# A hybrid encoder on one core: another PSUM bank for the pool sums, four mixer weights split early, GpSimd's work beside the recurrence moved to VectorE and ScalarE

## The chip, the core and the metric

The kernel runs on one core of a Trainium2 chip. Its engines are TensorE (PE, matmuls; PEld is its weight load), VectorE (DVE), ScalarE (ACT), GpSimd (POOL) and SyncE (SP, which here only issues DMAs). The metric is the device time of one execution in microseconds (us).

## The reference

A two-layer encoder for 256 tokens of width 1024, all in float32. Each layer is a mixer and a feed-forward part. The mixer makes one input projection and gives its columns to three head groups; their outputs are concatenated, projected back and added:

```python
h = rmsnorm(x, norm_mix[l])
proj = h @ w_in_first                      # layer 1: w_in_rest, with 32 more columns, v_down
u_rwkv, q, k, v, u_pool = split_cols(...)
y_a, v_first = rwkv7_mixer(u_rwkv, ...)    # bidirectional recurrence, 4 heads x 64
y_b = diff_attention(q, k, v, ...)         # partial rotary, 4 heads
y_c = pool_mixer(u_pool, ...)              # centred means over windows 2, 4, 8, 16
x = x + concatenate([y_a, y_b, y_c]) @ w_out[l]
x = x + (swiglu(h2, ffn...) if l == 0 else moe_swiglu(h2, router, exp...))   # h2 = rmsnorm(x)
```

In the recurrence `us = u + mu0 * (prev - u) + mu1 * (next - u)` is the shifted input. A decay `w` and a rate `a` come from two small low-rank projections (here "LoRA") of it, `kk` is the normalised key, and in layer 1 the value is mixed with that of layer 0: `v = v + (v_first - v) * sigmoid(vres_bias + v_down @ vres_up)` (the value residual). The feed-forward part of layer 0 is a dense SwiGLU (width 3584), that of layer 1 a mixture of 8 such experts.

## The kernel before, in words

**Stages.** Mixer 0 runs to 202 us of the span, the dense feed-forward part to 438, mixer 1 to 628, the experts to 1544.

**A weight's way.** A matmul in float32 precision is made of three passes on rounded operands (`mm3`): high by high, high by low, low by high. Each weight tile of 128x1024 (512 KB) therefore goes through `wload` (L184): SP loads `raw` (a ring of 4 slots), ACT rounds it to `whi` (L201, the "cast"), and DVE, or for the loads whose index is in `POOLW` GpSimd, computes `wlo = raw - whi` (L209, the "split"). `whi` and `wlo` have rings of 3 slots, so the split of a later weight waits until the matmuls of an earlier one are through. `self.spare` holds extra tiles that come ahead of the ring. They are parts of tiles which the mixer needs only later (`qk`, `qT`, `kT`), under the same tags. In layer 0 there are two, in layer 1 none. The index counts the mixer's loads after the first projection: in mixer 0, 0 and 1 are the two pool weights p0 and p1, 2 to 5 are q0 to q3, then k0 and so on; in mixer 1, 0 is `v_down`, 1 and 2 are p0 and p1, 3 to 6 are q0 to q3.

**A mixer up to the first Gram.** The first projection fills four PSUM banks (`pa`). DVE scales each into `u` (L552), and `us` is made of it with an ACT or GpSimd product and two DVE instructions for each of 8 columns (L546 to L550). PE then makes the LoRA products (`ps<-us,lora`), and between these and what follows the pool sums (p0, p1) and the projection q (q0 to q3). From the LoRA products DVE makes the scans of the decay (L631, L633). PE's sums of k squared (`ps<-consts,ksq`) go through DVE and GpSimd (`rn`, L621, L622) to `ksq` (L624), are transposed on PE and give `kk` (L642), `kd` (L659), `bb` (L657) and with the exponentials of the scans `Wd` and `IW` the operands `AR` (L655, and L656 on GpSimd) and `BK` (L665, L666). The Gram matmuls of direction 0 (`ps<-AR,BK`) need all of these for direction 0; the recurrence follows behind them.

**The order.** PE's order is written by hand: the parts of a mixer are generators which are woven, each `yield LAT[i]` being the modelled time after which the generator may go on. On the other engines a scheduler of the framework orders the instructions, so an edit can move instructions that it doesn't name.

**The value residual** (`vres`, mixer 1) and the pool sums both take a bank of tag `pq`. `vres` stands ahead of the pool sums in `proj`; behind its wait `LAT[15]` come the `vup` matmuls, a tanh on ACT, and four GpSimd instructions (L1038 to L1041).

## Time and profile before

| | |
|---|---|
| three runs, us | 1544.89, 1545.96, 1548.17; median 1545.96 |
| the profiled execution, us | 1545.79, of which the span of the profile is 1544.0 |
| PE busy | 1458.9 us, 94% of the span |
| DVE busy | 1002.7 us, 65% |
| ACT busy | 808.8 us, 52% |
| POOL busy | 176.5 us, 11% |
| DMA | 434.67 MB, 282 GB/s on average, about 410 GB/s in the experts |

The shares are averages over stages with different limits, so the stage must be looked at by itself.

### The profile page before, as it was taken

What the parts mean: (1) busy time and instruction counts of PE and PEld (TensorE: products, weight loads), DVE (VectorE), ACT (ScalarE), POOL (GpSimd) and SP (SyncE); (2) the same over time, 40 slices, a digit from 0 to 9 for tenths busy, and PEclk for the clock granted to TensorE, in tenths of its full rate; (3) what the DMA queues carried; (4) which work ended last, traced back from release to release, by engine and by line L of the source; (5) the groups of instructions that cost most, each with busy time, mean ns of one, the idle gap of its engine ahead of it and who ended that gap; (6) DMA issues with size and microseconds to landing.
All of it is one profiled execution on the core that took longest, in us unless ns stands there. A gap on an engine that the chain in (4) does not pass through costs nothing.

```text
span 1544.0 us, 27158 instructions
## 1 busy us (share of the span) xinstructions
PE 1458.9 (94%) x10215; PEld 1105.8 (72%) x10215; DVE 1002.7 (65%) x1314; ACT 808.8 (52%) x1142; POOL 176.5 (11%) x161
## 2 busy tenths in 40 slices
PE   6899989999998899899999999999999999998996
PEld 6777889999986768688743688888634787435885
DVE  4875665555659746799620898999512898206896
ACT  4545464444445354588510777777302776205785
POOL 2532100000026332400000000010000010000001
PEclk9899999999998899999999999999999999999998
DMA  7322255666543236779799999999999999999990
GB/s 228 108 71 98 98 176 178 190 190 187 170 121 96 61 135 247 259 275 363 283 413 414 411 411 411 411 388 339 368 419 411 410 411 417 409 416 411 410 411 36
DMA packets 172457, 434.67 MB, mean 282 GB/s; under 512 B 14834, under 2 KB 18013, under 8 KB 172317
## 3 DMA queue, kind: packets, MB, share of 16 engines
q1 hardware_dynamic: 170924, 430.74, 75.1%
q8 instruction: 82, 1.34, 0.3%
q0 software_dynamic: 544, 1.12, 0.3%
q10 hardware_dynamic: 848, 0.99, 0.3%
q14 instruction: 59, 0.48, 0.1%
HBM read 431.75 MB, written 1.05 MB: 280 GB/s over the span
## 4 chain that ended last, share of the span: by engine, by line
PE 73%; DMA 10%; DVE 10%; ACT 3%; issue 2%; POOL 1%; ACTq 0%; SPq 0%; DVEq 0%; POOLq 0%
PE ps L226 70%; DMA r<-in_exp_up 6%; PE ps L230 3%; DMA r<-in_exp_gate 2%; DVE wlo L209 1%; DVE wlox L209 1%; DMA lamk<-in_lambda_k 1%; ACT whi L201 1%; DMA r<-in_exp_down 1%; ACT whix L201 1%; DVE us L550 1%; DVE us L549 0%; DMA x<-in_x 0%; DVE BK L665 0%; ACT Sf L761 0%
## 5 line engine op out<-in xcount | busy, mean ns | idle before, releaser
L209 DVE TENSOR_TENSOR wlo<-r,whi 128x1024 fp32r<-128x1024 f32 x193 | 233.5, 1237 | 43.2 <-ACT whi L201 36.7
L201 ACT CAST whi<-r 128x1024 fp32r<-128x1024 f32 x196 | 202.6, 1054 | 37.3 <-DMA r<-in_exp_gate 18.5
L209 DVE TENSOR_TENSOR wlox<-r,whix 128x1024 fp32r<-128x1024 f32 x125 | 152.2, 1237 | 62.7 <-ACT whix L201 56.1
L201 ACT CAST whi<-raw 128x1024 fp32r<-128x1024 f32 x123 | 129.3, 1053 | 94.5 <-PE ps L226 82.8
L209 DVE TENSOR_TENSOR wlo<-raw,whi 128x1024 fp32r<-128x1024 f32 x108 | 137.2, 1273 | 56.5 <-ACT whi L201 56.0
L201 ACT CAST whix<-r 128x1024 fp32r<-128x1024 f32 x125 | 130.2, 1056 | 39.4 <-DMA r<-in_exp_gate 26.8
L226 PE MATMUL ps<-whi,gf 128*128 128x512 f32 x396 | 133.5, 395 | 0.0
L226 PE MATMUL ps<-r,gs 128*64 128x512 f32 (+1 forms) x636 | 131.1, 549 | 1.7 <-DMA r<-in_exp_up 1.7
L226 PE MATMUL ps<-fT,whi 128*128 128x256 f32 x544 | 98.5, 284 | 4.7 <-DVE gu L1306 3.8
L226 PE MATMUL ps<-whix,gf 128*128 128x512 f32 x276 | 95.3, 399 | 2.6 <-ACT whix L201 2.6
L226 PEld LDWEIGHTS ps<-r,gs 128*64 128x64 f32 x636 | 42.6, 136 | 72.4 <-issue 58.0
L1417 POOL TENSOR_TENSOR xp<-x,xp 128x512 fp32r<-128x512 f32 x12 | 22.3, 1858 | 626.9 <-ACT xp L1416 581.0
L226 PEld LDWEIGHTS ps<-fT,whi 128*128 128x128 f32 x544 | 84.4, 191 | 6.0 <-issue 4.3
L226 PEld LDWEIGHTS ps<-whi,gf 128*128 128x128 f32 x396 | 74.4, 188 | 18.2 <-issue 1.6
L1663 ACT COPY mah<-ps 128x512 f32<-128x512 f32 (+1 forms) x12 | 6.4, 532 | 139.5 <-PE ps L230 139.5
L226 PE MATMUL ps<-wlo,gf 128*128 128x512 f32 x198 | 78.1, 394 | 0.3 <-DVE wlo L209 0.2
L226 PE MATMUL ps<-fT,wlo 128*128 128x256 f32 x272 | 76.9, 283 | 0.0
L226 PE MATMUL ps<-whi,hT_h 128*128 128x512 f32 x160 | 70.4, 440 | 5.7 <-DVE up L1073 5.6
L209 DVE TENSOR_TENSOR wlox<-raw,whix 128x1024 fp32r<-128x1024 f32 x49 | 61.2, 1251 | 17.7 <-ACT whix L201 17.6
L226 PE MATMUL ps<-whi,mah 128*128 128x512 f32 x170 | 66.5, 391 | 0.0
L226 PE MATMUL ps<-wlo,hT_h 128*128 128x512 f32 x160 | 65.7, 410 | 0.8 <-DVE wlo L209 0.8
L226 PE MATMUL ps<-wlo,mah 128*128 128x512 f32 x170 | 66.4, 390 | 0.0
(460 smaller groups left out, 3376.7 us busy)
## 6 DMA issues: line engine op xcount, KB each, us to landing
r<-in_exp_gate SPq DMA_DIRECT2D x184, 512.0 KB, 10.0
r<-in_exp_up SPq DMA_DIRECT2D x173, 512.0 KB, 9.9
r<-in_exp_down SPq DMA_DIRECT2D x171, 512.0 KB, 10.1
raw<-in_exp_down SPq DMA_DIRECT2D x48, 512.0 KB, 10.0
raw<-in_exp_up SPq DMA_DIRECT2D x43, 512.0 KB, 10.0
raw<-in_exp_gate SPq DMA_DIRECT2D x34, 512.0 KB, 10.0
raw<-in_w_in_first SPq DMA_DIRECT2D x22, 512.0 KB, 4.4
raw<-in_w_in_rest SPq DMA_DIRECT2D x22, 512.0 KB, 3.7
```

What stands on the lines that cost most here:

```text
L201: w1 = nc.scalar.copy(hi[:, :a * b], raw[:, :a * b])
L209: w2 = (early or nc.vector).tensor_sub(lo[:, :a * b], raw[:, :a * b], hi[:, :a * b].bitcast(F32))
L226: self.nc.tensor.matmul(out, lhsT, rhs, start=start, stop=stop, skip_group_check=skip_group_check)
L230: self.nc.tensor.transpose(out, in_, ident)
L550: nc.vector.scalar_tensor_tensor(us[:, f, :T - 1], b[:, 1:], m1, us[:, f, :T - 1], op0=ALU.mult, op1=ALU.add)
L1417: nc.gpsimd.tensor_sub(xl, xs, xh.bitcast(F32))
L1663: nc.scalar.copy(at, b)
```

## The change

Four edits, all in the mixers:

- `POOLW` loses 5 and 6: the splits of q3 and k0 in mixer 0, of q2 and q3 in mixer 1, go from GpSimd to DVE.
- The spare tiles are now four for each of `whi` and `wlo`, in both layers: for `whi` the tile of tag `qk` and the first halves of `kT`, `AR` and `bkuv`, for `wlo` that of `qT` and the second halves. So the first four weights behind the first projection (p0, p1, q0, q1 in mixer 0; `v_down`, p0, p1, q0 in mixer 1) no longer wait for a slot of the ring, and `AR` and `BK` of the recurrence now wait for the matmuls of the weights that lie in their tiles.
- The pool sums take a bank of tag `at` instead of `pq`, and the `vup` matmuls of the value residual, with all that hangs on them, are written behind the pool sums instead of ahead of them.
- The zero halves of `kT` are written by ACT (a copy with scale 0) instead of by two GpSimd memsets.

```diff
-POOLW = (5, 6, 9, 12, 13, 14, 16, 22, 23)
+POOLW = (9, 12, 13, 14, 16, 22, 23)
...
-        if l == 0:
-
-            kT = P.tile([128, 2, 1024], F32R, name="kTs", tag="kT")
-            self.spare = {n: [P.tile([128, 1024], F32R, name=t_ + "s", tag=t_), kT[:, i_]]
-                          for i_, (n, t_) in enumerate((("whi", "qk"), ("wlo", "qT")))}
+
+        two = [P.tile([128, 2, 1024], F32R, name=t_ + "s", tag=t_) for t_ in ("kT", "AR", "bkuv")]
+        self.spare = {n: [P.tile([128, 1024], F32R, name=t_ + "s", tag=t_)] + [t2[:, i_] for t2 in two]
+                      for i_, (n, t_) in enumerate((("whi", "qk"), ("wlo", "qT")))}
...
-        yield LAT[15]
+        yield
         b = self.bank("pq")
...
-        if l > 0:
-            yield from self.vres(l, P, S["us"], hh, hl, wk)
-
-        pbk = self.bank("pq")
+        vres = self.vres(l, P, S["us"], hh, hl, wk) if l else iter(())
+        next(vres, 0)
+
+        pbk = self.bank("at")
...
+        next(vres, 0)
         self.S["up"] = up = P.tile([128, 3, 2, T + 2 * POOL_PAD], F32, name="up", tag="BKt")
...
-                nc.gpsimd.memset(tT[64:128, 0], 0.0)
-                nc.gpsimd.memset(tT[0:64, 1], 0.0)
+                for m in range(2):
+                    h = slice(64 - 64 * m, 128 - 64 * m)
+                    nc.scalar.activation(tT[h, m], self.rst[h, None, :].to_broadcast([64, 4, T]), AF.Copy, scale=0.0)
```

What the scheduler makes of it is seen in the order of the engines. DVE's queue in mixer 0, from the split of p1 (into `kTs`) on, before (`wlo_608` is of q0, `wlo_646` of q1; `ps_172` to `ps_175` are the four banks of the first projection):

```order
L209 TENSOR_TENSOR kTs<-raw_573,kTs 128x1024
L209 TENSOR_TENSOR wlo_608<-raw_606,whi_607 128x1024
L372 TENSOR_TENSOR ang<-ang 128x16
L373 TENSOR_SCALAR cos<-ang 128x16
L552 TENSOR_TENSOR u<-ps_172,R 128x512
L209 TENSOR_TENSOR wlo_646<-raw_644,whi_645 128x1024
L549 SCALAR_TENSOR_TENSOR us<-u,vecs,us 128x255
L552 TENSOR_TENSOR u<-ps_173,R 128x512
```

and with the change (`ARs` and `bkuvs` are the spare tiles, of q0 and q1; line numbers here are one lower):

```order
L209 TENSOR_TENSOR kTs<-raw_575,kTs 128x1024
L209 TENSOR_TENSOR ARs<-raw_608,ARs 128x1024
L372 TENSOR_TENSOR ang<-ang 128x16
L209 TENSOR_TENSOR bkuvs<-raw_644,bkuvs 128x1024
L373 TENSOR_SCALAR cos<-ang 128x16
L551 TENSOR_TENSOR u<-ps_172,R 128x512
L551 TENSOR_TENSOR u<-ps_173,R 128x512
L551 TENSOR_TENSOR u<-ps_174,R 128x512
L551 TENSOR_TENSOR u<-ps_175,R 128x512
L548 SCALAR_TENSOR_TENSOR us<-u,vecs,us 128x255 x2
```

The split of q1 moved ahead of the first scaling `u`, and the four scalings stand together.

DVE's queue in mixer 1, from the split of the first projection's weight number 6 on, before (`wlo_5132` is of its last weight, number 7, `wlo_5162` of `v_down`, `wlo_5169` of p0):

```order
L209 TENSOR_TENSOR wlo_5102<-raw_5100,whi_5101 128x1024
L209 TENSOR_TENSOR wlo_5132<-raw_5130,whi_5131 128x1024
L209 TENSOR_TENSOR wlo_5162<-raw_5160,whi_5161 128x1024
L552 TENSOR_TENSOR u<-ps_4909,R 128x512
L209 TENSOR_TENSOR wlo_5169<-raw_5167,whi_5168 128x1024
L549 SCALAR_TENSOR_TENSOR us<-u,vecs,us 128x255
L552 TENSOR_TENSOR u<-ps_4910,R 128x512
```

and with the change (`qTs` is of `v_down`, `kTs` of p0, `wlo_5130` of weight 7, `ARs` of p1, `bkuvs` of q0, `wlo_5400` of q1):

```order
L209 TENSOR_TENSOR wlo_5100<-raw_5098,whi_5099 128x1024
L209 TENSOR_TENSOR qTs<-raw_5163,qks 128x1024
L209 TENSOR_TENSOR kTs<-raw_5168,kTs 128x1024
L209 TENSOR_TENSOR wlo_5130<-raw_5128,whi_5129 128x1024
L209 TENSOR_TENSOR ARs<-raw_5299,ARs 128x1024
L209 TENSOR_TENSOR bkuvs<-raw_5363,bkuvs 128x1024
L209 TENSOR_TENSOR wlo_5400<-raw_5398,whi_5399 128x1024
L551 TENSOR_TENSOR u<-ps_4907,R 128x512
L551 TENSOR_TENSOR u<-ps_4908,R 128x512
```

Two splits now stand ahead of that of weight 7, and three more ahead of the first `u`.

GpSimd's queue in mixer 1, from its last product of `us` to the sum of `kd`, before:

```order
L1039 TENSOR_TENSOR vdf<-vfirst,us 128x512
L813 TENSOR_SCALAR sg<-us 128x2x2x64
L1038 TENSOR_SCALAR vsig<-vsig 128x512
L1040 TENSOR_TENSOR vdf<-vdf,vsig 128x512
L1041 TENSOR_TENSOR us<-us,vdf 128x512
L809 COPY vs<-us 128x4x2x64
L656 TENSOR_TENSOR AR<-us,Wd 128x8x64
L673 COPY wcx<-Wd 128x2 x3
L622 TENSOR_TENSOR rn<-rn,dvecs 128x8
L656 TENSOR_TENSOR AR<-us,Wd 128x8x64
L209 TENSOR_TENSOR wlo_5469<-raw_5467,whi_5468 128x1024
L209 TENSOR_TENSOR wlo_5487<-raw_5485,whi_5486 128x1024
```

and with the change:

```order
L1038 TENSOR_TENSOR vdf<-vfirst,us 128x512
L812 TENSOR_SCALAR sg<-us 128x2x2x64
L655 TENSOR_TENSOR AR<-us,Wd 128x8x64
L621 TENSOR_TENSOR rn<-rn,dvecs 128x8
L672 COPY wcx<-Wd 128x2 x3
L655 TENSOR_TENSOR AR<-us,Wd 128x8x64
L672 COPY wcx<-Wd 128x2 x3
L1037 TENSOR_SCALAR vsig<-vsig 128x512
L1039 TENSOR_TENSOR vdf<-vdf,vsig 128x512
L1040 TENSOR_TENSOR us<-us,vdf 128x512
L808 COPY vs<-us 128x4x2x64
L675 TENSOR_TENSOR kd<-kd 128x512
```

The two splits are gone from it, and the value residual's instructions went behind the `AR` products and `rn`. From the first Gram on, the orders of all engines agree but for a few places, and SP's agrees throughout.

## Rows read from the trace of the kernel before

**Rows 1.** The page: the span, and ACT's casts (count, busy, mean ns).

```profile
span 1544.0 us, 27158 instructions
...
L201 ACT CAST whi<-raw 128x1024 fp32r<-128x1024 f32 x123 | 129.3, 1053 | 94.5 <-PE ps L226 82.8
```

**Rows 2.** Windows: length; busy of PE, PEld, DVE, ACT, POOL; granted clock; DMA.

```profile
42.30:72.50 30.20, 22.69 (x115) 18.82 (x113) 28.23 (x40) 16.35 (x32) 20.70 (x19) 0.86 0.30 89
71.00:77.60 6.60, 5.12 (x33) 4.93 (x33) 5.74 (x10) 0.00 (x0) 1.88 (x2) 0.50 0.28 82
464.60:498.80 34.20, 26.84 (x146) 22.57 (x144) 32.37 (x42) 20.14 (x36) 23.20 (x20) 0.85 0.30 91
498.80:502.10 3.30, 3.27 (x33) 3.18 (x34) 3.30 (x6) 0.00 (x0) 1.27 (x1) 1.00 0.56 162
628.00:1544.00 916.00, 881.95 (x4081) 598.55 (x4079) 602.50 (x634) 509.29 (x617) 39.93 (x24) 0.99 0.95 371
```

**Rows 3.** Chain of waits, 40 to 80 us: start, length, what.

```profile
68.02 2.77 DVE AR L655
```

**Rows 4.** Timeline of DVE in mixer 0: start, length, what, idle before and its releaser.

```profile
41.30 0.68 DVE L552 TENSOR_TENSOR u<-ps,R 128x512 f32<-128x512 f32 x1
42.44 1.30 DVE L209 TENSOR_TENSOR wlo<-raw,whi 128x1024 fp32r<-128x1024 f32 x1 [0.45 <-ACT whi L201]
...
52.75 1.26 DVE L631 TENSOR_TENSOR_SCAN cs<-rst,cs 128x256 f32<-128x256 f32 x2
...
60.56 1.41 DVE L624 COPY ksq<-rn 128x512 f32<-128x512 f32 x1 [1.79 <-POOL rn L622]
61.89 0.68 DVE L659 TENSOR_TENSOR kd<-kd,us 128x512 f32<-128x512 f32 x1
...
63.21 2.88 DVE L659 TENSOR_TENSOR kd<-kd,us 128x512 f32<-128x512 f32 x1
...
67.94 2.85 DVE L655 TENSOR_TENSOR AR<-kk,Wd 128x512 f32<-128x512 f32 x1
```

**Rows 5.** Timeline of POOL in mixer 0.

```profile
62.70 2.84 POOL L209 TENSOR_TENSOR wlo<-raw,whi 128x1024 fp32r<-128x1024 f32 x1
```

**Rows 6.** Timeline of PE in mixer 0.

```profile
46.08 2.83 PE L226 MATMUL ps<-us,lora 128*128 128x256 f32 x12 [0.87 <-issue]
...
57.07 1.49 PE L226 MATMUL ps<-consts,ksq 128*128 128x2 f32 x8
...
72.47 5.10 PE L226 MATMUL ps<-AR,BK 64*128 64x128 f32 x32 [3.84 <-DVE BK L665]
```

**Rows 7.** Timeline of DVE in mixer 1.

```profile
458.75 1.23 DVE L209 TENSOR_TENSOR wlo<-raw,whi 128x1024 fp32r<-128x1024 f32 x1 [1.49 <-ACT whi L201]
...
464.60 0.69 DVE L552 TENSOR_TENSOR u<-ps,R 128x512 f32<-128x512 f32 x1 [1.30 <-PE ps L226]
...
478.40 3.38 DVE L631 TENSOR_TENSOR_SCAN cs<-rst,cs 128x256 f32<-128x256 f32 x2
...
489.89 2.74 DVE L666 TENSOR_TENSOR BK<-kd,IW 128x512 f32<-128x512 f32 x1
...
496.09 2.93 DVE L665 TENSOR_TENSOR BK<-bb,IW 128x256 f32<-128x256 f32 x2
```

**Rows 8.** Groups of DVE's instructions, 464.6 to 498.8 us: count, busy, mean ns, idle.

```profile
L209 DVE TENSOR_TENSOR wlo<-raw,whi 128x1024 fp32r<-128x1024 f32 x4 | 4.8, 1207 | 0.0
```

**Rows 9.** Timeline of POOL in mixer 1.

```profile
478.28 1.32 POOL L1040 TENSOR_TENSOR vdf<-vdf,vsig 128x512 f32<-128x512 f32 x1
```

**Rows 10.** Timeline of SP's DMA issues in mixer 1.

```profile
454.57 0.38 SPq L198 DMA_DIRECT2D raw<-in_w_in_rest  x1
...
460.00 0.37 SPq L198 DMA_DIRECT2D raw<-in_w_in_rest  x1
```

**Rows 11.** DMA issues, 425 to 530 us: count, KB each, median us to landing.

```profile
raw<-in_w_in_rest SPq DMA_DIRECT2D x17, 512.0 KB, 3.7
```

**Rows 12.** Timeline of PE in mixer 1.

```profile
498.83 3.20 PE L226 MATMUL ps<-AR,BK 64*128 64x128 f32 x32 [1.62 <-DVE BK L665]
```

## The prediction

> **What bounds the kernel now.** I read the windows by stage first [rows 2]. The experts, the last 916 of 1544 us, keep the DMA engines 0.95 busy at 371 GB/s: their end moves only if their beginning does. No edit touches them or the dense part, and the orders behind the first Gram agree, so the change is worth what it shifts the first Gram of either mixer. In the 30.2 us ahead of the first, DVE is busy 28.23, PE 22.69. In the 34.2 us in mixer 1 it is 32.37 against 26.84. There DVE is the limit: its work, not a wait, sets the Gram, and the two Grams' idle time names DVE's `BK` as releaser [rows 6, 12].
>
> The chain of waits says which DVE work. On it lies `AR` with 2.77 us [rows 3], an instruction of a form that takes 0.68 elsewhere. The timeline of DVE shows why: `kd` takes 0.68 at 61.89 and 2.88 at 63.21, `AR` 2.85 [rows 4], and the long `kd` ends within 0.6 us of the split that GpSimd began at 62.70 [rows 5]. When a two-input GpSimd instruction runs beside a two-input DVE instruction, the DVE one lasts until the other ends. In mixer 1 two `BK` take 2.74 and 2.93 in the same way, and the pair of L631 scans 3.38 [rows 7] beside the value residual's products [rows 9], where the pair in mixer 0 takes 1.26 [rows 4].
>
> The clock comes third: it is granted at 0.50 (the level of 1.2 GHz) from 71 to 77.6 us and at 1.00 (2.4 GHz) from 498.8 on [rows 2]. PE had waited 3.84 us in the first case and 1.62 in the second, and the same 32 Gram matmuls take 5.10 and 3.20 us [rows 6, 12].
>
> **The change part by part, mixer 0.**
>
> *The opening.* q1's split, which ends at 43.7 [rows 4], now stands ahead of the first `u`, so the four `u` run from 43.7, 0.6 us apart. The work is the same, but what filled the wait ahead of that split (one `u`) comes behind it: +0.6 on DVE. The pool sums' bank is now one of the first projection's, free after the third `u` (43.7 + 3 x 0.6 = 45.5), where before PE went on at 42.3. So PE idles 3.2 us, a wait that the change adds, and behind it in PE's hand-written order stand the pool sums of p0 (24 matmuls; before they filled 42.3 to 45.2, where the 0.87 of idle ahead of the LoRA matmuls begins [rows 6]) and the LoRA matmuls: 45.5 + 2.7 = 48.2, with ACT's tanh behind k0's cast (1.05 [rows 1]) some 48.9 instead of 46.08, +2.8. Who waits for LoRA is the first scan (52.75 [rows 4]). LoRA ends at 50.0 before, 52.8 after, just as DVE comes to it: covered. What stands next on PE is p1, six matmuls of q0 and the sums of k squared, at 57.07 before [rows 6]. The wait of q for the pool sums' bank goes away with the other tag, so they stand there again: 52.8 + 2.7 (24 matmuls, as for p0) + 1.4 (six of twice that width) = 56.9. `rn` and DVE's idle time ahead of `ksq` stay where they were; the opening's 0.6 is spent there. Term: 0, at worst +1.5.
>
> *From `ksq` (60.56) to the Gram (72.47).* Gone are the excesses of `kd` (2.88 - 0.68 = 2.2) and of `AR` (2.85 - 0.68 = 2.2), since the two splits have left GpSimd. The splits stand on DVE instead. k0's goes into the 1.79 us in which DVE waits for `rn` [rows 4], at nothing; with that cover gone it would cost 1.2. q3's costs 1.2. The second `AR` and the second `BK` of `kd` (0.6 each) now come behind the Gram's operands: -1.2. GpSimd's `AR` product must wait until q0's matmuls have left its tile and lands beside `kd`, as a two-input instruction of about the length of that in [rows 9] (1.32): +1.0, between 0 and 1.3. Sum: -2.2 - 2.2 + 1.2 - 1.2 + 1.0 = -3.4. If k0's and q3's splits both find idle time and the `AR` product costs nothing it is -5.6. On the other side PE decides: 18 matmuls of q stand between the transposes of `ksq` and the Gram, and PE was through with them 3.84 us ahead of it [rows 6], so at full clock the Gram can come 3.8 earlier; at half clock those 18 take up to 4.1 longer (18 x 0.23, twice the 2.7 / 24 of a pool matmul of half the width), and little is gained; I bound it at -1.3.
>
> *The clock.* With the Gram at 69 PE has waited some 0.5 us ahead of it instead of 3.84. Then it should run as that of mixer 1, 3.20 instead of 5.10: -1.9, and the q matmuls behind it at full clock too, though the inverses behind those are DVE's. I take -2, between 0 and -3.7 (all of the low stretch of 6.6 us [rows 2], and some more behind it).
>
> Mixer 0: -3.4 - 2.0 = **-5.4**.
>
> **Mixer 1.** *The opening.* Before, SP issued q0's load at 460.00, when the split of weight 7 (458.75 + 1.23) freed its raw slot [rows 7, 10]. Now ACT and DVE take `v_down` and p0 ahead of weight 7. p0's load, issued at 454.57, lands 3.7 later [rows 10, 11], at 458.3; then come p0's cast and `R`, the cast of weight 7 and its split: 458.3 + 1.4 + 1.05 + 1.2 = 462. PE wants that weight at about 464, so the projection is not held up. But q0's load is issued 2.0 later, lands at 462 + 3.7 = 465.7, and two casts (q0, q1) and two splits follow before DVE may start the first `u`: 465.7 + 1.05 + 1.2 + 1.2 = 469.2 instead of 464.6. This is the price of the spare tiles: +4.6, from 0 (if the scheduler's order were not to wait) to 5.5. Queued behind it are all `us`, LoRA and GpSimd's products. Against it, four splits (4.8 us [rows 8]) were done within the stretch and now stand ahead of it: -4.8. So the opening is worth about nothing.
>
> *GpSimd.* The two splits of q2 and q3 go to DVE, +2.4; the `BK` excesses go, 2.74 - 0.68 + 2.93 - 0.75 = 4.2 (0.75 is a pair of half width, by the 0.68 of one whole): -4.2. The value residual's instructions leave the scans, 3.38 - 1.26 = -2.1, and some 1.6 that they and their neighbours cost other instructions there. They come, with the `AR` products and `vs`, beside `kd`, `BK` and `AR`: five instructions at about 1.0 each, +5. Balance: +1.3. `up` goes into the wait for `rn`: -0.6.
>
> Mixer 1: +4.6 - 4.8 + 2.4 - 4.2 + 1.3 - 0.6 = **-1.3**, from -4.5 (the opening costs 2 less, half of the five cost nothing) to +1.5.
>
> The zero halves of `kT` cost ACT one instruction each half, about 1 us in all (a cast of 128x1024 takes 1.05 [rows 1]), ahead of the exponentials for `AR`. ACT is busy 16.35 of 30.2 and 20.14 of 34.2 us [rows 2] and waits for the scans there, so I put it at nothing; without that cover it is +1 in either mixer.
>
> **Sum**: -5.4 - 1.3 = -6.7, and the profiled execution took 1545.79, within 0.2 of the median of its three runs: 1539. Its own range is 1534 to 1543.
>
> **The rivals.**
>
> *More.* The opening of mixer 1 costs nothing net and the splits find idle time: mixer 0 -7.6, mixer 1 -4.5, so 1533.7. For it speaks that DVE idles 1.30 and 1.79 us ahead of `u` and `ksq` [rows 4, 7]; against it, that every one of those waits then has to be the right one.
>
> *No change.* GpSimd's excess is moved, not removed. The five instructions in mixer 1 cost their whole 1.3 (+1.5 more), and in mixer 0 PE, not DVE, is last, at half clock (-1.3 there, nothing for the clock): -1.3 + 0.2, so 1544.7. For it speaks that the excess in every row is nearly the whole of the other's length; against it, that PE had already waited 3.84 us for DVE in mixer 0 [rows 6]. By the Trainium skill, "SBUF — State Buffer", section "Who interferes with whom", a DVE instruction with two inputs in SBUF and a GpSimd one that reads it exclude each other for a whole instruction; the long rows of `kd`, `AR` and `BK` agree. By that rule each of the five moved instructions costs its whole length, the +1.5 of this rival; with the rest of the forecast unchanged that is 1540.6.
>
> *Slower.* The two new waits of PE (3.2 us at 42.3; in mixer 1 about as long, since `v_down`'s bank now waits for the first `u`) bring the clock down, as 3.84 us did at 71 [rows 2, 6]. Then pool sums and LoRA run at 0.50 and take 6.6 us longer; DVE covers about 2.5 of it in mixer 0, and the sums of k squared, `rn` and the Gram come 4 later. That eats the 5.4 there but for 1.4, and in mixer 1 +4 against -1.3 leaves +2.7; with the opening at its upper bound and the clock low at the Gram as well (+2) it is +3.5: 1549.3. It decides once the sums of k squared end later than 62 us. Against it: 1.62 us of waiting left the clock at 1.00 in mixer 1 [rows 12], and the new waits lie between 1.62 and 3.84, nearer the latter. The Trainium skill, "TensorE: Matmul & The Clock Gate", section "Why this matters for your kernels", warns that idle gaps between bursts of matmuls bring the engine back to its lower speed; the one long wait above agrees, and by that rule 1549.3 would be the time.
>
> **How the numbers follow.** The forecast has 0.50, more 0.15, no change 0.24, slower 0.11. A measurement of this kernel tells 0.2%, 3.1 us: faster is below 1542.9, slower above 1549. The forecast's range reaches that limit, so a little of its 0.50 goes to "same" and a little of the no-change case to "faster": 0.66, 0.24, 0.10. The range leaves out the slower case and what lies beyond the larger gain: 1532 to 1547.
>
> **What would show it.** Right: `kd`, `AR` and `BK` of 0.68 to 1.4 us in DVE's timeline ahead of both Grams; the first Gram near 69 us in about 3.2 us; the first `u` of mixer 1 near 469 and its Gram near 497 less the 5.4 of mixer 0. Wrong: `ksq` matmuls after 60 us in mixer 0, or a clock below 1.00 from 45 to 55 us (the slower case); GpSimd's products as the longest neighbours of `kd` and `BK` (no change); a difference that arises behind the Grams, which I have put at nothing, would prove the method itself wrong.

## The result, and the profile after

The changed kernel takes 1537.04 us (median of five runs, 1533.59 to 1538.05) against 1545.96 for the kernel before (five runs now, 1544.89 to 1548.17). The ratio is 0.9937, its 95% interval 0.9923 to 0.9951. The medians differ by 8.9 us, where about 7 (1539, range 1532 to 1547) was forecast. The profiled execution took 1537.17 us. The page of it, with the span and the busy time of each engine:

```profile
span 1535.4 us, 27152 instructions
...
PE 1454.0 (95%) x10215; PEld 1102.3 (72%) x10215; DVE 996.8 (65%) x1318; ACT 812.5 (53%) x1146; POOL 163.7 (11%) x153
```

PE has the same 10215 matmuls. Its busy time fell by 4.9 us (from 1458.9) and its idle time by 3.7 (1544.0 - 1458.9 = 85.1 before, 81.4 now). The matmuls are the same, so more than half of the 8.6 us of span is matmuls that ran at a higher clock, not waits that got shorter. The forecast had 2 us of that, at another place.

Where the difference arises, from the starts of single instructions in the traces (the last column is a second profile of the changed kernel, experiment 5; `nr` is the first instruction of mixer 1's normalisation, `cmp` the experts' first). The Gram can start on a part of its operands, so there is a second mark: the first inverse matmul (`ps<-inv,inv`; the recurrence inverts 32x32 blocks that are made of the Gram), which comes behind the whole Gram of direction 0.

| start of, us | before | changed | changed, again |
|---|---|---|---|
| the first `u` of mixer 0 | 41.30 | 44.08 | 44.72 |
| the first Gram matmul of mixer 0 | 72.47 | 68.89 | 69.54 |
| the first inverse matmul of mixer 0 | 84.99 | 80.91 | 82.58 |
| `nr` (L378) at the entry to mixer 1 | 441.52 | 437.35 | 438.71 |
| the first `u` of mixer 1, after that `nr` | 23.08 | 28.43 | 29.04 |
| the first Gram of mixer 1, after that `nr` | 57.32 | 52.46 | 52.99 |
| the first inverse of mixer 1, after that `nr` | 68.98 | 66.34 | 66.52 |
| the experts' first `cmp` (L1443), after that `nr` | 186.33 | 179.76 | 180.34 |
| the end, after that `cmp` | 916.17 | 918.28 | 915.73 |

Mixer 0 with the dense part gained 4.2 us (2.8 in the second profile), mixer 1 6.6 (6.0), and the experts lost 2.1 (gained 0.4). The forecast had 5.4, 1.3 and 0. Cut at the first inverses, in us:

| stretch | forecast | measured | again |
|---|---|---|---|
| to the first inverse of mixer 0 | -5.4 | -4.1 | -2.4 |
| from there to `nr` | 0 | -0.1 | -0.4 |
| from `nr` to the first inverse of mixer 1 | -1.3 | -2.6 | -2.5 |
| from there to `cmp` | 0 | -3.9 | -3.5 |
| the experts | 0 | +2.1 | -0.4 |
| sum | -6.7 | -8.6 | -9.2 |

The largest piece that the forecast lacked lies behind the first inverse of mixer 1. These windows go from there to the last inverse matmul of that mixer (length; busy of PE, PEld, DVE, ACT, POOL; granted clock; DMA), in the kernel before, the changed kernel and its second profile:

```profile
510.50:566.30 55.80, 52.29 (x1323) 42.40 (x1324) 32.24 (x67) 26.93 (x55) 17.55 (x14) 0.91 0.34 111
503.70:555.60 51.90, 48.04 (x1325) 38.08 (x1324) 31.25 (x67) 26.97 (x55) 17.22 (x14) 1.00 0.37 118
505.20:557.50 52.30, 48.17 (x1324) 38.22 (x1324) 31.62 (x67) 26.95 (x55) 17.59 (x14) 1.00 0.37 117
```

The stretch is 3.9 and 3.5 us shorter, PE's busy time in it 4.3 and 4.1, at a clock of 1.00 instead of 0.91.

The timeline of DVE in mixer 0, which answers to [rows 4]:

```profile
44.08 2.48 DVE L551 TENSOR_TENSOR u<-ps,R 128x512 f32<-128x512 f32 x4
...
58.08 1.22 DVE L209 TENSOR_TENSOR wlo<-raw,whi 128x1024 fp32r<-128x1024 f32 x1
...
59.29 1.21 DVE L209 TENSOR_TENSOR wlo<-raw,whi 128x1024 fp32r<-128x1024 f32 x1
62.08 1.41 DVE L623 COPY ksq<-rn 128x512 f32<-128x512 f32 x1 [1.58 <-POOL rn L621]
63.41 2.47 DVE L658 TENSOR_TENSOR kd<-kd,us 128x512 f32<-128x512 f32 x2
...
66.52 0.69 DVE L654 TENSOR_TENSOR AR<-kk,Wd 128x512 f32<-128x512 f32 x1
...
68.33 1.82 DVE L664 TENSOR_TENSOR BK<-bb,IW 128x256 f32<-128x256 f32 x2
```

The pair of `kd` takes 2.47 us where its two instructions took 3.56, `AR` 0.69 where it took 2.85. Behind it, PE (the timeline that answers to [rows 6]):

```profile
46.10 0.36 PE L226 MATMUL ps<-hT_h,qks 128*128 128x256 f32 x1 [3.74 <-DVE u L551]
...
50.53 3.61 PE L226 MATMUL ps<-us,lora 128*128 128x256 f32 x16
...
58.20 0.95 PE L226 MATMUL ps<-consts,ksq 128*128 128x2 f32 x8
...
68.89 0.46 PE L226 MATMUL ps<-AR,BK 64*128 64x128 f32 x2 [0.54 <-DVE BK L664]
70.21 2.04 PE L226 MATMUL ps<-AR,BK 64*128 64x128 f32 x22 [0.86 <-DVE BK L664]
72.61 1.16 PE L226 MATMUL ps<-AR,BK 64*128 64x128 f32 x8 [0.37 <-DVE G L709]
```

The new wait for the pool sums' bank is there (3.74 us), LoRA is 4.4 us later, and the Gram nevertheless starts 3.6 earlier, behind a wait of 0.54. It starts with two matmuls on the first half of `BK`; then PE waits 0.86 for the other half and 0.37 for DVE's `G`. So its 32 matmuls take 4.9 us from first to last (68.89 to 73.77), at a clock of 1.00, hardly less than the 5.10 of before [rows 6]. In mixer 1, DVE before and after (against [rows 7]):

```profile
477.11 1.37 DVE L628 TENSOR_SCALAR cs<-cs 128x512 f32<-128x512 f32 x2
...
481.70 2.56 DVE L633 TENSOR_TENSOR_SCAN cs<-rst,cs 128x256 f32<-128x256 f32 x2
...
487.25 1.41 DVE L624 COPY ksq<-rn 128x512 f32<-128x512 f32 x1 [1.79 <-POOL rn L622]
```

```profile
464.64 1.22 DVE L209 TENSOR_TENSOR wlo<-raw,whi 128x1024 fp32r<-128x1024 f32 x1
465.78 1.28 DVE L551 TENSOR_TENSOR u<-ps,R 128x512 f32<-128x512 f32 x2
...
475.97 0.75 DVE L627 TENSOR_SCALAR cs<-cs 128x512 f32<-128x512 f32 x2
476.64 1.42 DVE L630 TENSOR_TENSOR_SCAN cs<-rst,cs 128x256 f32<-128x256 f32 x2
477.98 1.24 DVE L632 TENSOR_TENSOR_SCAN cs<-rst,cs 128x256 f32<-128x256 f32 x2
479.14 3.32 DVE L209 TENSOR_TENSOR wlo<-raw,whi 128x1024 fp32r<-128x1024 f32 x2
...
484.33 0.43 DVE L623 COPY ksq<-rn 128x512 f32<-128x512 f32 x1 [1.19 <-POOL rn L621]
...
488.84 2.23 DVE L664 TENSOR_TENSOR BK<-bb,IW 128x256 f32<-128x256 f32 x2
```

and GpSimd beside it (against [rows 9]):

```profile
479.67 1.71 POOL L655 TENSOR_TENSOR AR<-us,Wd 128x512 f32<-128x512 f32 x1 [2.15 <-ACT Wd L633]
...
489.48 1.31 POOL L1039 TENSOR_TENSOR vdf<-vdf,vsig 128x512 f32<-128x512 f32 x1
```

The scans take 1.42 instead of 3.38, and the value residual's products start when the first half of that `BK` is done, at the time of the Gram's start (489.81): they cost what comes behind that start, not what comes ahead of it.

### The profile page after: what moved, and what is told of

Same layout as the page of the kernel before. It is cut to its first block, busy times and chain, and to the rows that moved or that the text cites. A ratio compares the mean times of both kernels' runs of the same rounds, so it can differ in the third digit from the quotient of the medians.

```text
span 1535.4 us, 27152 instructions
## 1 busy us (share of the span) xinstructions
PE 1454.0 (95%) x10215; PEld 1102.3 (72%) x10215; DVE 996.8 (65%) x1318; ACT 812.5 (53%) x1146; POOL 163.7 (11%) x153
## 4 chain that ended last, share of the span: by engine, by line
PE 73%; DVE 10%; DMA 9%; ACT 4%; issue 3%; POOL 1%; ACTq 0%; SPq 0%; DVEq 0%; POOLq 0%
PE ps L226 71%; DMA r<-in_exp_up 5%; PE ps L230 3%; DMA r<-in_exp_gate 2%; DVE wlo L209 2%; DVE wlox L209 1%; DMA lamk<-in_lambda_k 1%; ACT whi L201 1%; DMA raw<-in_w_in_rest 1%; DVE us L549 0%; ACT whix L201 0%; DVE us L548 0%; ACT nsq L389 0%; DMA x<-in_x 0%; ACT hT_h L409 0%
## 5 line engine op out<-in xcount | busy, mean ns | idle before, releaser
L201 ACT CAST whi<-raw 128x1024 fp32r<-128x1024 f32 x117 | 123.1, 1054 | 95.9 <-PE ps L226 86.0
L209 DVE TENSOR_TENSOR wlo<-raw,whi 128x1024 fp32r<-128x1024 f32 x106 | 133.9, 1267 | 55.0 <-ACT whi L201 54.5
L226 PE MATMUL ps<-whi,mah 128*128 128x512 f32 x170 | 66.5, 391 | 0.0
L226 PE MATMUL ps<-whi,mal 128*128 128x512 f32 x170 | 66.2, 389 | 0.0
L226 PE MATMUL ps<-r,mah 128*64 128x512 f32 x264 | 63.8, 600 | 2.3 <-DMA r<-in_exp_down 1.8
```

The lines of the kernel that those rows point to most:

```text
L201: w1 = nc.scalar.copy(hi[:, :a * b], raw[:, :a * b])
L209: w2 = (early or nc.vector).tensor_sub(lo[:, :a * b], raw[:, :a * b], hi[:, :a * b].bitcast(F32))
L226: self.nc.tensor.matmul(out, lhsT, rhs, start=start, stop=stop, skip_group_check=skip_group_check)
```

## The experiments

Every kernel was compared with the kernel before on its chip; the interval is of that ratio. One execution of each was profiled. The stages of all of them, as in the table above, and the length of the stretch from the first to the last inverse of mixer 1 with its granted clock (before: 55.8 us at 0.91; changed: 51.9 at 1.00):

| kernel | median, us | ratio (interval) | Gram, inverse of mixer 0 | Gram, inverse of mixer 1 after `nr` | inverses of mixer 1 (clock) | `cmp` after `nr` |
|---|---|---|---|---|---|---|
| 1 splits back on GpSimd | 1542.43 | 0.9973 (0.9958 to 0.9989) | 71.15, 82.49 | 55.15, 67.19 | 57.1 (0.89) | 185.83 |
| 2 spare tiles as before | 1541.39 | 0.9955 (0.9937 to 0.9972) | 68.47, 80.67 | 52.52, 68.97 | 56.7 (0.94) | 187.20 |
| 3 bank and value residual as before | 1546.96 | 0.9994 (0.9977 to 1.0012) | 69.68, 83.40 | 58.62, 69.21 | 58.3 (0.88) | 189.01 |
| 4 before, only the splits moved | 1545.13 | 0.9976 (0.9962 to 0.9990) | 68.00, 79.86 | 54.87, 68.71 | 59.1 (0.88) | 189.34 |
| 5 the changed kernel again | 1538.66 | 0.9943 (0.9924 to 0.9962) | 69.54, 82.58 | 52.99, 66.52 | 52.3 (1.00) | 180.34 |
| 6 before, 22 filler matmuls | 1545.75 | 0.9994 (0.9980 to 1.0008) | 73.73, 83.91 | 57.88, 69.55 | 55.4 (0.91) | 186.47 |
| 7 changed, filler in mixer 1 | 1539.14 | 0.9945 (0.9928 to 0.9963) | 68.41, 81.79 | 55.64, 69.54 | 51.5 (0.97) | 182.61 |
| 8 changed, value residual ahead | 1542.09 | 0.9968 (0.9955 to 0.9982) | 69.66, 82.77 | 54.52, 66.21 | 58.3 (0.86) | 186.09 |
| 9 changed, `u` first in mixer 1 | 1540.91 | 0.9960 (0.9944 to 0.9976) | 68.52, 81.70 | 53.49, 67.33 | 54.0 (0.97) | 182.87 |
| 10 changed, `u` first in both | 1547.08 | 0.9991 (0.9976 to 1.0006) | 69.15, 84.72 | 52.36, 66.20 | 54.9 (0.94) | 182.67 |
| 11 `kT` zeros back on GpSimd | 1546.46 | 0.9991 (0.9975 to 1.0006) | 67.10, 80.81 | 54.71, 66.75 | 58.3 (0.86) | 186.65 |
| 12 before, 13 filler matmuls | 1542.81 | 0.9969 (0.9957 to 0.9982) | 74.97, 85.23 | 57.30, 68.96 | 56.1 (0.88) | 186.57 |

A profile shows one execution, and not always a typical one: those of experiments 1, 2 and 12 lie 5.9 to 6.6 us above the median of their kernel, those of 10 and 11 3.2 and 3.7 below it.

### 1. Without the moved splits

```diff
-POOLW = (9, 12, 13, 14, 16, 22, 23)
+POOLW = (5, 6, 9, 12, 13, 14, 16, 22, 23)
```

> The changed kernel with the splits of q3 and k0 (mixer 0) and q2 and q3 (mixer 1) put back on GpSimd, the three other edits kept. Theory (a two-input instruction on GpSimd stretches the two-input DVE instruction beside it, and that is what bounded the stretch ahead of the Gram): the long DVE rows come back ahead of both Grams, about 2.2 us each less the two splits of 1.2 us that DVE loses, of which one lay in idle time: some 2 to 3 us later in mixer 0 and 1 to 2 in mixer 1, so 1540 to 1542. Rival (the early splits into the spare tiles are what gained): no change against the changed kernel, 1537.

By the ratios the kernel is about 5 us above the changed one (0.9973 against 0.9937 and 0.9943), where the theory had 3 to 5. The place is another: the two splits now stand ahead of `rn` on GpSimd and hit the scans. GpSimd and DVE in mixer 0:

```profile
54.71 5.50 POOL L209 TENSOR_TENSOR wlo<-raw,whi 128x1024 fp32r<-128x1024 f32 x2
```

```profile
55.20 5.56 DVE L632 TENSOR_TENSOR_SCAN cs<-rst,cs 128x256 f32<-128x256 f32 x2
```

Two scans that take 1.24 us together in the changed kernel end within 0.6 us of the second split, 4.3 us late. In this run, where GpSimd's instruction falls decides who pays, not whether somebody does.

### 2. Without the spare tiles

```diff
-        two = [P.tile([128, 2, 1024], F32R, name=t_ + "s", tag=t_) for t_ in ("kT", "AR", "bkuv")]
...
+        if l == 0:
```

> The changed kernel with the spare tiles as before (two in layer 0, none in layer 1). Theory: the four early splits only move DVE work from behind the first u to ahead of it, so mixer 0 stays within 1 us and in mixer 1 the first u comes 2 to 5 us earlier while the four splits of 1.2 us go back behind it: 1535 to 1539. Rival (the spare tiles are what gained): the gain of mixer 1, 6.6 us behind the dense part, falls by half or more: 1541 or later.

The median is between the two, 2 to 3 us above the changed kernel; the intervals of the ratios overlap, so the times don't separate it. In the profile both Grams start as early as with the tiles (68.47, and 52.52 after `nr`), as the theory has it for the openings. But the first inverse of mixer 1 comes 68.97 after `nr`, as in the kernel before, and 2.5 us later than in the changed kernel: two splits now stand on DVE between the Gram's start and it (500.81 and 504.31, 1.21 and 1.30 us), where the changed kernel has one (497.35). Behind it another 4 to 5 us are lost at a clock of 0.94. So the rival is right for mixer 1 up to the first inverse, in part for a reason that neither theory named. What is lost behind it is that of the slowest of six executions (1547.47, the others 1538.54 to 1542.43), and the median has room for the first part alone.

### 3. Without the bank and the value residual's place

```diff
-        yield
+        yield LAT[15]
...
-        vres = self.vres(l, P, S["us"], hh, hl, wk) if l else iter(())
-        next(vres, 0)
...
-        pbk = self.bank("at")
+        if l > 0:
+            yield from self.vres(l, P, S["us"], hh, hl, wk)
...
+        pbk = self.bank("pq")
...
-        next(vres, 0)
```

> The changed kernel with the pool sums' bank of tag pq again and the value residual ahead of the pool sums. Theory: in mixer 0 PE no longer waits 3.7 us for the bank but q waits for the pool sums' bank again, and the Gram stays within 1 us; in mixer 1 the value residual's GpSimd instructions return beside the scans, and the scans and what follows get 3 to 4 us longer: 1540 to 1541. Rival (the place of the value residual doesn't matter, since the same GpSimd instructions only move): 1537, and the scans of 3.4 us are answered by shorter rows behind them.

Worse than either: 0.9994, no gain left. The Gram of mixer 1 comes 58.62 after `nr`, 6.2 later than in the changed kernel and later than before (57.32). The value residual's place and the bank's tag were put back together here; experiment 8 takes them apart.

### 4. Only the splits moved

```diff
-POOLW = (5, 6, 9, 12, 13, 14, 16, 22, 23)
+POOLW = (9, 12, 13, 14, 16, 22, 23)
```

> The kernel before with only the four splits moved from GpSimd to DVE. Theory: kd and AR of mixer 0 and the two BK of mixer 1 take 0.7 to 1.4 us instead of 2.7 to 2.9; with the splits on DVE paid for, 2 to 3 us gained in mixer 0 and 1 to 2 in mixer 1: 1541 to 1543. Rival (the edits only work together, since DVE is the bound and gets 4 more splits of 1.2): 1545 to 1547.

DVE in both mixers:

```profile
63.10 0.69 DVE L659 TENSOR_TENSOR kd<-kd,us 128x512 f32<-128x512 f32 x1
...
65.64 0.68 DVE L655 TENSOR_TENSOR AR<-kk,Wd 128x512 f32<-128x512 f32 x1
...
475.99 3.38 DVE L631 TENSOR_TENSOR_SCAN cs<-rst,cs 128x256 f32<-128x256 f32 x2
```

`kd` and `AR` went from 2.88 and 2.85 to 0.69 and 0.68 [rows 4], and the Gram of mixer 0 comes 4.5 us earlier by this edit alone, its first inverse 5.1: that GpSimd's splits held DVE in mixer 0 is shown. In mixer 1 the scans keep their 3.38, and the Gram starts 2.4 earlier. At the first inverse 0.3 of that is left, for two splits now stand on DVE between the two (498.84 and 502.50, 2.14 and 1.35 us) where before there was one (504.51, 1.21). Behind it 3.3 us are lost at a clock of 0.88. By the ratio the kernel gained 3.7 us, within the theory's 3 to 5; by the bare median, 1545.13, it would be the rival's.

### 5. The changed kernel again

```diff
 (no change)
```

> The changed kernel once more, on the chip of the three runs beside it, to see what of its first profile stays from execution to execution. Theory (the waits are set by the orders, the low stretches of the clock are not): the first Grams of both mixers come at the same distance from the start of their mixer within 1 us, but the low clock from 439 to 446 us and the others may be missing or stand elsewhere; the times spread by some 5 us and lie lower where the mean granted clock is higher. Rival (the clock follows from the waits): the same low stretches at the same places.

The Grams stay within 1 us, as the theory had it; the times spread by 7.8 us (1534.54 at a mean clock of 0.984, 1542.30 at 0.973). Of the clock both had a part. Windows of the second profile (length; busy of PE, PEld, DVE, ACT, POOL; clock; DMA):

```profile
440.00:448.00 8.00, 6.92 (x35) 6.95 (x36) 3.81 (x11) 3.86 (x8) 5.90 (x13) 0.57 0.39 119
71.00:79.00 8.00, 8.00 (x40) 7.01 (x41) 7.58 (x14) 0.81 (x2) 2.32 (x2) 0.57 0.01 2
```

The low stretch at the entry to mixer 1 is the same as in the first profile, that from 71 to 79 us isn't in the first.

### 6 and 12. Filler ahead of the first Gram, in the kernel before

```diff
             b = self.bank("pr")
+            if d == 0 and hd == 0 and l == 0:
+                self.warm(b, 22)
```

`warm` writes that many matmuls of the identity with itself into the bank, which the Gram then overwrites; in experiment 12 there are 13.

> The kernel before, with 22 matmuls of the identity with itself put into the first bank of the first Gram, ahead of it, in mixer 0 alone; the Gram overwrites them. They fill the 3.84 us in which PE waited for BK and wait for nothing themselves. Theory (the Gram's 5.10 us and the low clock from 71 to 82 us came of that wait): the clock stays at 1.00, the Gram takes about 3.2 us and mixer 0 is 2 to 4 us shorter with no DVE row changed, 1543 to 1545. Rival (the low clock came for another reason, or the time behind the Gram is DVE's anyhow): no change beyond 1 us.

> The kernel before with 13 instead of 22 matmuls of the identity ahead of the first Gram of mixer 0 (22 of them took 5.1 us, more than the wait of 3.84; 13 should take 3.0). Theory (the clock's share in the gain of mixer 0 is about 2 us): the Gram begins where it did, 72.5, takes 3.2 instead of 5.1 us, and the dense part begins 1 to 2 us earlier. Rival (behind the Gram DVE and the inverses set the pace, and the low clock comes a little later anyhow): the dense part begins within 1 us of before.

PE with 22 of them (the records count two for each):

```profile
68.73 5.07 PE L226 MATMUL ps<-ident 128*128 128x128 f32 x44
73.73 2.26 PE L226 MATMUL ps<-AR,BK 64*128 64x128 f32 x24
```

and a window behind:

```profile
87.00:98.00 11.00, 11.00 (x107) 9.91 (x106) 5.69 (x15) 3.03 (x6) 1.55 (x2) 0.53 0.15 47
```

The first 24 of the Gram's 32 records take 2.26 us, at full clock, yet the low stretch that stood at 71 to 82 us (0.54) stands at 87 to 98 instead, and with 13 at 88 to 99. In both kernels the first inverse comes 1.4 us earlier, counted from the first `u` (42.3 against 43.7). Then it is lost: with 22 the dense part's first `silu` comes 0.8 us earlier than before, the rival's answer, and by the times nothing is gained. With 13 the fillers end ahead of `BK`, and in the profile the first `silu` of the dense part comes 185.4 us after the first `u` of mixer 0, against 183.0 before: no gain. But that profile is of the slowest of its twelve executions (1549.38), and by the times this kernel is 0.31% faster than the one before, eight executions lying between 1541.95 and 1543.08. That is half of what the whole change gains, from a filler alone. What the short filler gains there, the profile doesn't show; it stays open.

### 7. Filler at the entry to mixer 1

```diff
+        for i in range(3 * l):
+            self.warm(self.bank("pr"), 4)
         pa = self.banks4()
```

> The changed kernel with 12 matmuls of the identity with itself (into three banks that nothing reads) ahead of the first projection of mixer 1, where PE waits about 2.1 us for the normalised input. Theory: the low clock from 439 to 446 us of the first profile is gone in every execution, the first projection ends 2.85 us earlier against the start of the mixer, and the kernel gains up to 2.8 us on the executions that had it, 1 to 2 in the median. Rival (loads and splits, not PE, set the first u of mixer 1): the projection gets shorter but the first u and the Gram stay within 1 us.

This one missed its aim. The fillers waited for the same `hT_l` (2.05 us), so they stood behind the wait and made it longer: the projection began 6.36 us after `nr` instead of 2.37, and the first `u` came 30.15 after it. It says nothing on either theory.

### 8. The value residual ahead, the bank of tag `at` kept

```diff
-        yield
+        yield LAT[15]
...
-        vres = self.vres(l, P, S["us"], hh, hl, wk) if l else iter(())
-        next(vres, 0)
+        if l > 0:
+            yield from self.vres(l, P, S["us"], hh, hl, wk)
...
-        next(vres, 0)
```

> The changed kernel with the value residual ahead of the pool sums again, the pool sums' bank staying that of tag at. Theory (what I put too small is the place of the value residual's GpSimd instructions): mixer 0 as in the changed kernel; in mixer 1 the first Gram comes 3 to 5 us later, since rn and the AR products on GpSimd stand behind the value residual, and the median is 3 to 5 us above that of the changed kernel. Rival (the bank did it): within 1 us of the changed kernel.

In time as the theory said: 3.4 us above experiment 5, which ran on the same chip. GpSimd in mixer 1,

```profile
478.12 1.54 POOL L1039 TENSOR_TENSOR vdf<-vdf,vsig 128x512 f32<-128x512 f32 x1
479.74 1.54 POOL L1040 TENSOR_TENSOR us<-us,vdf 128x512 f32<-128x512 f32 x1
```

and DVE:

```profile
477.54 2.67 DVE L632 TENSOR_TENSOR_SCAN cs<-rst,cs 128x256 f32<-128x256 f32 x2
480.13 3.78 DVE L209 TENSOR_TENSOR wlo<-raw,whi 128x1024 fp32r<-128x1024 f32 x2
...
486.24 1.40 DVE L623 COPY ksq<-rn 128x512 f32<-128x512 f32 x1 [2.25 <-POOL rn L621]
```

The scans behind pay 1.4 (2.67 against 1.24), the splits 0.5, `ksq` 1.0, the wait for `rn` 1.1: about 4. The Gram starts 1.5 to 2.1 later, not 3 to 5, for the first `u` comes 2.5 to 3.1 earlier: the first projection runs in 23.0 us here and in 25.6 and 26.1 in the two profiles of the changed kernel, where the clock is low. From `u` to the first inverse the stretch is 2.4 to 2.8 longer, and that inverse comes no later than in the changed kernel (66.21 against 66.34 and 66.52). The loss in the profile lies behind it, 58.3 us for the inverses where the changed kernel takes 52:

```profile
505.70:564.00 58.30, 55.02 (x1322) 44.58 (x1324) 32.33 (x67) 27.09 (x55) 17.50 (x14) 0.86 0.33 104
```

PE has the same matmuls there, 6.9 us more busy time, and a clock of 0.86 instead of 1.00. So what the place of the value residual costs DVE is shown, but not that the 3.4 us are this cost. Experiment 3, which differs from it by the bank's tag alone, is another 0.26% slower by the ratios.

### 9 and 10. The first `u` ahead of the late splits

```diff
-                nc.scalar.activation(us[:, f], b, AF.Copy, scale=dv[:, i:i + 1])
+                o = nc.scalar.activation(us[:, f], b, AF.Copy, scale=dv[:, i:i + 1])
+                if f == 6 and l:
+                    self.hi_after = o.ins
...
+            if n_ == 0 and l:
+                self.after = o.ins
```

In the lines left out, `o` is also the scaling `u`, and both names are cleared at the end of the mixer. Later casts are queued behind `hi_after`, later splits behind `after`. Experiment 10 has this without `and l`, so in both layers.

> The changed kernel, where in mixer 1 the splits of the weights behind p0 are queued behind the first u on DVE, and their casts behind the first product of us on ACT. Theory (the opening's price, the first u waiting for the late loads of q0 and q1, is real, and what DVE idles there can be had back): the first u comes 23 to 24 us behind the start of the mixer instead of 28.4, three splits of 1.2 us return behind it, and the first Gram of mixer 1 comes 1.5 to 3 us earlier: 1 to 3 us below the changed kernel. Rival (the splits only move, and DVE has the same work ahead of the Gram): the Gram stays within 1 us.

> As the kernel beside it, in both mixers. Theory: in mixer 0 PE's wait for the pool sums' bank falls from 3.7 to about 1 us, but the sums of k squared already stand ahead of DVE's rn by about 1 us, so the Gram of mixer 0 gains at most 1 us. Rival (that wait of PE sets LoRA and so the scans): the Gram of mixer 0 comes 2 us or more earlier.

DVE in mixer 1 of experiment 9:

```profile
462.25 1.40 DVE L553 TENSOR_TENSOR u<-ps,R 128x512 f32<-128x512 f32 x2 [2.79 <-PE ps L226]
...
476.74 1.19 DVE L209 TENSOR_TENSOR bkuvs<-raw,bkuvs 128x1024 fp32r<-128x1024 f32 x1
```

The first `u` comes 24.46 after `nr` instead of 28.4 to 29.0, the splits return behind it (`bkuvs` is shown, `ARs` and q1's are others), and the Gram comes 53.49 after `nr` instead of 52.5 to 53.0, the first inverse 67.33 instead of 66.3 to 66.5: the rival. Where the splits stand, ahead of `u` or behind, is worth less than 1 us, as the forecast's balance of the opening (+4.6 - 4.8) said. In mixer 0 of experiment 10, PE and then DVE:

```profile
69.15 3.10 PE L226 MATMUL ps<-AR,BK 64*128 64x128 f32 x32
...
77.52 0.80 PE L226 MATMUL ps<-wlo,hT_h 128*128 128x512 f32 x1 [4.84 <-DVE wlo L209]
```

```profile
70.34 0.69 DVE L714 TENSOR_TENSOR G<-ps,consts 128x512 f32<-128x512 f32 x1 [2.19 <-PE ps L226]
```

LoRA comes 4.2 us earlier than in the changed kernel, the Gram not, as the theory said: it starts without a wait, and now DVE waits for PE. That is the bound from PE's side that the forecast put at the other end of its term. Behind it k0's split is late, PE waits 4.84 us for it, and the first inverse of mixer 0 comes 2 to 4 us later than in the changed kernel. No kernel here is shown to be faster than the changed one.

### 11. The zeros of `kT` on GpSimd

```diff
-                for m in range(2):
-                    h = slice(64 - 64 * m, 128 - 64 * m)
-                    nc.scalar.activation(tT[h, m], ..., AF.Copy, scale=0.0)
+                nc.gpsimd.memset(tT[64:128, 0], 0.0)
+                nc.gpsimd.memset(tT[0:64, 1], 0.0)
```

> The changed kernel with the zero halves of kT written by two memsets on GpSimd again. Theory: a memset doesn't stretch DVE's instructions (1.20 us for a split beside one in mixer 0 before), and ACT hid its two fills: within 1.5 us of the changed kernel, the first Grams within 0.7 us. Rival (GpSimd's queue is what rn and the AR products wait in): the memsets of about 1 us each come ahead of rn, and each Gram comes 1 to 2 us later.

Both were wrong: the Gram of mixer 0 is 1.8 us earlier than in the first profile of the changed kernel, that of mixer 1 2.2 later, as the rival had it for both, and the ratio is 0.9991. GpSimd and DVE in mixer 1:

```profile
474.10 0.95 POOL L1158 MEMSET kT<- 64x1024 f32 x1 [0.18 <-POOL vdf L1038]
...
475.54 0.94 POOL L1159 MEMSET kT<- 64x1024 f32 x1
```

```profile
474.12 2.64 DVE L627 TENSOR_SCALAR cs<-cs 128x512 f32<-128x512 f32 x2
```

A pair that takes 0.75 us in the changed kernel takes 2.64 here and ends 0.3 us behind the second memset; between the two memsets GpSimd runs a `tensor_scalar` of 0.45 us. The Trainium skill, "SBUF — State Buffer", section "Who interferes with whom", says that a two-input DVE instruction isn't held by a GpSimd one that only writes, but that `tensor_scalar` can enter a mode that uses both ports and then excludes GpSimd. Both halves agree: this pair, and a split beside a memset in mixer 0 of the kernel before, GpSimd first:

```profile
54.27 1.11 POOL L1158 MEMSET kT<- 64x1024 f32 x1
```

```profile
54.41 1.20 DVE L209 TENSOR_TENSOR wlo<-raw,whi 128x1024 fp32r<-128x1024 f32 x1
```

The pair is 1.9 us. By the ratios the kernel is more than 7 us slower than the changed one, and the rest isn't explained by it: in the profile the first inverse of mixer 1 comes 0.2 to 0.4 later than in the changed kernel, though the first `u` comes 2.4 to 3.0 earlier, and the inverses take 58.3 us at a clock of 0.86.

## Why the prediction was right, and where not

**The number: near, and in part by luck.** 1537 lies in the range, 2 us from the forecast. But up to the first inverses the two profiles gained 6.7 and 4.9 us where the forecast had 6.7; mixer 0 gave less than forecast, mixer 1 more. Another 3.9 and 3.5 came behind the first inverse of mixer 1, at a higher clock, where the forecast had nothing.

**What bounds the stretch: right.** The long rows of `kd` and `AR` were the path in mixer 0, and taking the splits off GpSimd alone moves its first Gram by 4.5 us and its first inverse by 5.1 (experiment 4). In mixer 1 the same edit shortens the `BK` and leaves 0.3 at the first inverse.

**Mixer 0 to the Gram: right.** Forecast -3.4, measured -3.6 and -2.9. The new wait of PE was forecast at 3.2 and is 3.74; LoRA was forecast at 48.9 and came at 50.5, the sums of k squared at 58.2 instead of 56.9, still ahead of DVE's `rn` (59.2). As forecast, one of the two new splits stands ahead of DVE's `rn` (58.08) and one in the wait behind it (59.29). But GpSimd's `rn` beside that one takes 2.59 us instead of 1.68, so 1.58 of the wait stayed.

**The clock, -2: mis-sized.** The term let the Gram take 3.20 instead of 5.10. The Gram ran at full clock in the first profile and took 4.9 from its first to its last matmul, since it starts on the first half of `BK` and waits for DVE twice behind that. The second profile has the low stretch of 71 to 79 us behind the same wait (0.55); from the first `u` to the first inverse it takes 37.9 us, the first one 36.8. So the clock is worth 1.0 there, and 1.4 in experiments 6 and 12. In these two the low stretch came later instead. By its times experiment 12 gained 0.31% and experiment 6 nothing; why is open.

**Mixer 1, the opening: too dear, and near by luck.** Forecast +4.6 for the first `u`, measured 5.3 and 6.0. But the first projection ran at the low clock for a while in both profiles (0.51 and 0.57) and took 2.9 and 3.3 us longer. In experiments 1, 3, 8 and 11, which have the spare tiles and a faster projection (23.0 to 23.3 us against 22.8 before), the first `u` comes 25.95 to 26.33 after `nr`: the tiles cost about 3. That the opening costs nothing on balance is shown by experiment 9 within 1 us.

**Mixer 1, GpSimd's balance: the other term that was mis-sized.** I put it at +1.3: 3.7 us saved beside the scans, 5 paid beside `kd`, `BK` and `AR`. From `u` to the Gram's start the stretch fell by 10.2 us (34.2 to 24.0) where the terms made 5.9. The saving is larger, since not only the L631 scans but L628 (1.37 to 0.75), L633 (2.56 to 1.24) and `ksq` (1.41 to 0.43) had stood beside GpSimd's work: 0.6 + 2.0 + 1.3 + 1.0 = 4.9. And of what comes instead, only the `AR` products fall ahead of the Gram's start (the pair of splits takes 3.32 instead of 2.3, a `kd` 0.99 instead of 0.68: +1.3); the value residual's fall behind it, for the Gram starts on the first half of `BK`. There they are paid in part: from `u` to the first inverse the stretch fell by 8.0 and 8.4 (45.9 to 37.9 and 37.5). So the balance was some 2 us better than +1.3 there, not the 4 that the Gram's start shows.

**Mixer 1's bounds.** The lower one, -4.5, doesn't come out of its own items: 2 and half of 5 off -1.3 make -5.8. Measured at the first inverse: -2.6 and -2.5.

**`kT`'s zeros at nothing: wrong.** I asked what they cost ACT and forgot what they had cost beside GpSimd's new neighbours. Experiment 11: without this edit the other three gain 0.09%, inside the noise. The profile shows 1.9 us of that cost on DVE; most of the loss is not explained.

**Nothing behind the Grams: wrong.** The forecast called this a sign that would prove the method itself wrong, and it came. In mixer 1 the changed kernel loses some 2 us between the Gram's start and the first inverse and gains 3.9 and 3.5 behind that. Over all the profiles the stretch of the inverses goes with its clock: 51.5 to 54.0 us at 0.97 to 1.00, 54.9 to 59.1 at 0.86 to 0.94. It was 1.00 in both profiles of the changed kernel, and 0.91, 0.91 and 0.88 in the three kernels whose mixer 1 is that of before. Which edit brings the higher clock, and why, is not shown.

**The rivals.** "Slower" had its mechanism half right: at 46 to 50 us the clock is 0.57 behind the new wait, as these windows of the changed kernel show, one of the forecast's own signs of being wrong. But DVE covers it, and the sums of k squared ended at 59.2, ahead of the 62 that was to decide. The rule of the Trainium skill that was cited for it holds there (3.74 us of waiting, low clock), and 1549 didn't follow.

```profile
46.00:50.00 4.00, 3.90 (x20) 3.93 (x21) 4.00 (x10) 3.90 (x9) 2.40 (x2) 0.57 0.32 116
439.00:446.00 7.00, 6.28 (x30) 6.31 (x31) 2.89 (x9) 3.35 (x7) 5.25 (x10) 0.51 0.36 106
```

"No change" gives about the time of kernels 3 and 11. That GpSimd's excess, moved and not removed, makes it is shown for the rows above and argued for the rest.

## What to carry to other kernels

Where GpSimd works beside a DVE-bound stretch, list each of its instructions with the DVE instruction that runs beside it, before and after, and in the order that the scheduler makes; an edit that moves one of them is priced by its new neighbour. Edits that clear one stretch together should be costed together: here one of them alone gave 0.24%, three of the four next to nothing when the wrong one was missing (experiments 3 and 11), and all four 0.6%.

Measure a shift at an instruction that needs everything that was moved. The Gram starts on the first half of an operand; what landed behind that point seemed free at its start and was back, by some 2 us, at the first inverse.

## What the runs showed of the hardware

The same wait at the same place can leave the clock high or bring it low. At the entry to mixer 1 PE waits 2.12 us in the kernel before and goes on at 1.00; it waits 2.13 us in the changed one and goes on at 0.51, and so in the second profile (2.14 us of waiting, low clock). The first projection's matmuls take 2.85 and 3.3 us longer for it:

```profile
439.72 0.55 PE L226 MATMUL ps<-hT_h,whi 128*128 128x256 f32 x1 [2.13 <-DVE hT_l L412]
```

The spread of one kernel goes with it: of 35 executions of the kernel before on one chip, the eight with the highest mean granted clock (0.979 to 0.981) have a median of 1544.8 us, the eight with the lowest (0.972 to 0.974) 1550.9. A change of 0.2% can't be read from a few executions of this kernel; the stages of the profile tell more, as long as one looks at the clock of each stage too.

GpSimd is held as well: `rn` (L621), 1.68 us elsewhere, takes 2.59 in mixer 0 of the changed kernel, beside a split on DVE (59.29 to 60.50).
